# An L2 pool over four neighbours: fp32 throughout, 63 KB input runs in two slots, and the last stores queued behind the last load

## The chip, the cores and the metric

The kernel runs on one core of a Trainium2 chip. The metric is the device time of one execution in microseconds (us), the median of nine runs. ACT, DVE and SP stand for ScalarE, VectorE and SyncE; the core's 16 DMA engines move all data between device memory and SBUF.

## The reference

For x of shape 32 x 256 x 4096 in fp32, p = 2 and a window of 4, each output is the root of the mean of the squares of four neighbours along the last axis:

```python
for i in range(out_length):
    window = np.abs(x[:, :, i * 4:i * 4 + 4]) ** p
    result[:, :, i] = (np.mean(window, axis=-1)) ** (1.0 / p)
```

The input is 134.2 MB, the output (32 x 256 x 1024) 33.55 MB. Each byte is moved once.

## The kernel before

The input is seen as 8192 rows of 4096. The loop at L46 makes 32 tiles of 256 rows, two consecutive rows for each of the 128 partitions, so one partition's part of a tile is one run of 8192 elements (32 KB). The load of a tile (L50, 4 MB) is issued on SP's queue into one of three slots of `in_pool` (L42): the load of tile i + 3 waits on SP until the second square of tile i has read its slot.

A tile is worked in two halves of 4096 columns (L56). For each half ACT squares fp32 into bf16 (L60). DVE then adds in two steps: elements 0 and 1 of each group of four to elements 2 and 3 (L66, 2048 results in bf16, in `c`), then the two partial sums (L73, 1024 results, in `sum4`). ACT takes the root with the scale 1/4 (L78) into the fp32 output tile `ot`. After both halves the store of the tile (L84, 1 MB, 8 KB a partition) is issued on ACT's own queue, from one of four slots of `out_pool` (L44).

The order of instructions on each engine is set by the tile framework's scheduler from the program order and the dependencies. The trace shows the squares of a tile ahead of the root of the half before them where data are there. Two queues of DMA descriptors feed the same 16 engines: q1 holds SP's loads and q10 ACT's stores.

Of the kernel before, what the change touches and what calls it, by code (L numbers as in the profile page):

```python
# [1 line left out]

# [4 lines left out]


@with_exitstack
def kernel(  # L10
    ctx: ExitStack,
    tc: tile.TileContext,
    x: bass.AP,
    p: float,
    kernel_size: int,
    out: bass.AP,
):
    nc = tc.nc

    assert float(p) == 2.0, "kernel specialized for p == 2"  # L20
    k = int(kernel_size)
    assert k == 4, "kernel specialized for kernel_size == 4"

    x_flat = x.flatten_outer_dims()
    out_flat = out.flatten_outer_dims()
    R, L = x_flat.shape
    P = nc.NUM_PARTITIONS

    ROWS_PER_PART = 2
    CHUNK_ROWS = P * ROWS_PER_PART  # L30
    CL = L * ROWS_PER_PART
    CLo = CL // k
    assert R % CHUNK_ROWS == 0
    n_tiles = R // CHUNK_ROWS
    n_halves = 2
    HL = CL // n_halves
    HLo = HL // k

    fp32 = mybir.dt.float32
    bf16 = mybir.dt.bfloat16  # L40

    in_pool = ctx.enter_context(tc.tile_pool(name="in_pool", bufs=3))  # L42
    mid_pool = ctx.enter_context(tc.tile_pool(name="mid_pool", bufs=4))
    out_pool = ctx.enter_context(tc.tile_pool(name="out_pool", bufs=4))  # L44

    for i in range(n_tiles):  # L46
        rows = slice(i * CHUNK_ROWS, (i + 1) * CHUNK_ROWS)

        xt = in_pool.tile([P, CL], fp32)
        nc.sync.dma_start(  # L50
            out=xt,
            in_=x_flat[rows].rearrange("(p t) l -> p (t l)", t=ROWS_PER_PART),
        )

        ot = out_pool.tile([P, CLo], fp32)
        for h in range(n_halves):  # L56
            xh = xt[:, h * HL:(h + 1) * HL]

            x2 = mid_pool.tile([P, HL], bf16)
            nc.scalar.activation(  # L60
                out=x2, in_=xh, func=mybir.ActivationFunctionType.Square,
            )

            x2v = x2.rearrange("p (n j) -> p n j", j=k)
            c = mid_pool.tile([P, 2 * HLo], bf16)
            nc.vector.scalar_tensor_tensor(  # L66
                out=c.rearrange("p (n j) -> p n j", j=2),
                in0=x2v[:, :, 0:2], scalar=1.0, in1=x2v[:, :, 2:4],
                op0=mybir.AluOpType.mult, op1=mybir.AluOpType.add,
            )  # L70
            cv = c.rearrange("p (n j) -> p n j", j=2)
            sum4 = mid_pool.tile([P, HLo], bf16)
            nc.vector.scalar_tensor_tensor(  # L73
                out=sum4, in0=cv[:, :, 0], scalar=1.0, in1=cv[:, :, 1],
                op0=mybir.AluOpType.mult, op1=mybir.AluOpType.add,
            )

            nc.scalar.activation(  # L78
                out=ot[:, h * HLo:(h + 1) * HLo], in_=sum4,
                func=mybir.ActivationFunctionType.Sqrt,  # L80
                scale=1.0 / k,
            )

        nc.scalar.dma_start(  # L84
            out=out_flat[rows].rearrange("(p t) l -> p (t l)", t=ROWS_PER_PART),
            in_=ot,
        )


# [1 line left out]
_INS = ['x', 'p', 'kernel_size']  # L91
_OUTS = [((32, 256, 1024), 'float32')]
#: Inputs that are plain numbers.
_NUMBERS = {'p': 2.0, 'kernel_size': 4}


# [26 lines left out]
```

## Time and profile before

| what | value |
|---|---|
| median of 9 runs (lowest to highest) | 404.66 us (404.59 to 405.06) |
| the profiled execution: its time / its span | 404.75 us / 402.8 us |
| moved, and mean rate over the span | 167.80 MB, 417 GB/s |
| loads (L50): number, size, median from issue to landing | 32, 4096 KB, 28.3 us |
| stores (L84): number, size, median from issue to landing | 32, 1024 KB, 16.6 us |
| SP's queue waiting for ACT's squares (L60), in total | 228.6 us, 29 times |
| ACT idle ahead of the squares, for loads | 58.8 us |
| DVE idle ahead of the first add, for squares | 170.5 us |

A row of an instruction group reads: line, engine, operation, tile written <- tile read, shapes and types, number of instructions | busy time in all (us) and mean of one (ns) | idle time of the engine just ahead of them, and what ended it. A row of a busy-time table reads: the stretch and its length (us), busy time and instructions of DVE, ACT and POOL, the granted clock, the mean share of time in which a DMA engine held a packet, and GB/s. In the row of slices each digit is a fortieth of the span, 9 for 90% or more.

### The profile page before, as it was taken

The numbers are of one execution on the slowest core, as the hardware profiler recorded it, in microseconds if no ns is written. First come the engines' busy times: TensorE is split into PE (matmuls) and PEld (weight loads), VectorE is DVE, ScalarE is ACT, GpSimd is POOL, SyncE is SP. The second block draws the span as 40 slices with busy tenths as digits, with TensorE's granted clock in tenths as the row PEclk, the third lists the DMA queues.
The fourth block names the chain that finished last, engine by engine and source line by source line (L and its number), as shares of the span: only waits on it lengthen the run. The fifth ranks groups of instructions, "written<-read, shape, count | busy, mean of one in ns | idle before, by whom it ended". The sixth has DMA issues, their size and how long they took to land.

```text
span 402.8 us, 424 instructions
## 1 busy us (share of the span) xinstructions
DVE 224.3 (56%) x128; ACT 293.0 (73%) x130; POOL 0.2 (0%) x4
## 2 busy tenths in 40 slices
DVE  0357466645556654466554566455566554566454
ACT  1788777787676885767977677876767977677872
POOL 0000000000000000000000000000000000000000
DMA  8999999999999999999999999999999999999962
GB/s 355 426 428 405 443 446 403 440 456 403 456 413 433 443 434 423 451 402 448 438 414 448 422 428 448 432 418 451 404 446 440 417 443 432 418 448 414 430 257 104
DMA packets 9219, 167.80 MB, mean 417 GB/s; under 512 B 1024, under 2 KB 1024, under 8 KB 1024
## 3 DMA queue, kind: packets, MB, share of 16 engines
q1 hardware_dynamic: 4608, 134.22, 77.4%
q10 hardware_dynamic: 4608, 33.56, 19.7%
q14 instruction: 3, 0.02, 0.0%
HBM read 134.22 MB, written 33.55 MB: 416 GB/s over the span
## 4 chain that ended last, share of the span: by engine, by line
DMA 58%; ACT 26%; DVE 9%; issue 6%; SPq 0%; ACTq 0%
DMA xt<-in_x_dram 58%; ACT x L60 22%; DVE c L66 6%; ACT ot L78 4%; DVE sum L73 3%; SPq L50 0%; ACTq L78 0%
## 5 line engine op out<-in xcount | busy, mean ns | idle before, releaser
L60 ACT ACTIVATE x<-xt 128x4096 bf16<-128x4096 f32 x64 | 229.1, 3604 | 58.8 <-DMA xt<-in_x_dram 58.8
L66 DVE SCALAR_TENSOR_TENSOR c<-x 128x2048 bf16<-128x2048 bf16 x64 | 146.7, 2292 | 170.5 <-ACT x L60 170.5
L78 ACT ACTIVATE ot<-sum 128x1024 f32<-128x1024 bf16 x64 | 67.1, 1049 | 45.5 <-DVE sum L73 43.8
L73 DVE SCALAR_TENSOR_TENSOR sum<-c 128x1024 bf16<-128x1024 bf16 x64 | 78.4, 1225 | 2.2
L60 ACT ACT_TABLE_LOAD x1 | 1.3, 1283 | 0.7 <-PEq L104 0.7
L78 ACT ACT_TABLE_LOAD x1 | 1.3, 1283 | 0.0
L104 POOL MEMSET const-bfloat16-1.0<- 128x1 bf16 x1 | 0.1, 101 | 0.0
L104 POOL MEMSET const-uint8-127<- 128x1 uint8 x1 | 0.1, 101 | 0.0
L104 POOL MEMSET const-float32-0.0<- 128x1 f32 x1 | 0.1, 98 | 0.2 <-issue 0.2
L104 POOL MEMSET const-float32-1.0<- 128x1 f32 x1 | 0.1, 98 | 0.0
## 6 DMA issues: line engine op xcount, KB each, us to landing
xt<-in_x_dram SPq DMA_DIRECT2D x32, 4096.0 KB, 28.3
out_dram<-ot ACTq DMA_DIRECT2D x32, 1024.0 KB, 16.6
```

Source lines behind the costliest of these rows:

```text
L60: nc.scalar.activation(out=x2, in_=xh, func=mybir.ActivationFunctionType.Square,)
L66: nc.vector.scalar_tensor_tensor(out=c.rearrange("p (n j) -> p n j", j=2), in0=x2v[:, :, 0:2], scalar=1.0, in1=x2v[:, :, 2:4], op0=mybir.A ...
L73: nc.vector.scalar_tensor_tensor(out=sum4, in0=cv[:, :, 0], scalar=1.0, in1=cv[:, :, 1], op0=mybir.AluOpType.mult, op1=mybir.AluOpType.add,)
L78: nc.scalar.activation(out=ot[:, h * HLo:(h + 1) * HLo], in_=sum4, func=mybir.ActivationFunctionType.Sqrt, scale=1.0 / k,)
L104: nc = _bacc.Bacc("TRN2", target_bir_lowering=False, num_devices=1)
```

## The change

The work is laid out anew over the flat input, 262144 elements for each of the 128 partitions.

- Fourteen big tiles of W = 16128 elements a partition (63 KB, one run each, 8.26 MB) go through two slots of `x_pool`. Two big tiles share one block of device memory, so that they have one output tile `ot` of 8064 elements a partition (32 KB) and one store of 4.13 MB.
- What is left, 36352 elements a partition, is the tail: four loads of H = 8064 elements (two to a slot) and one of END = 4096. The last load takes the slot of the first two, which must be worked off first; in the unused part of that slot lie the outputs of the last two groups.
- Everything is fp32. Squares and roots are taken in place. Of a big tile's four column blocks of CH = 4032, ACT squares three and a half and DVE half of the fourth (a plain multiply). DVE's two adds are plain tensor_tensor additions through a small scratch tile `s`.
- `manual_schedule` keeps the order of the program text on every engine. In it all squares of a big tile come first, then the adds, then the load of the tile after next (SP), then two roots of 2016 elements, and after every second big tile the store, on ACT's queue. In the tail the root of a block comes after the square of the next.
- The store of the last pair of big tiles and the two stores of the tail are issued on SP's queue, after the last load.

The diff, blank lines left out:

```diff
-    x_flat = x.flatten_outer_dims()
-    out_flat = out.flatten_outer_dims()
-    R, L = x_flat.shape
     P = nc.NUM_PARTITIONS
-    ROWS_PER_PART = 2
-    CHUNK_ROWS = P * ROWS_PER_PART
-    CL = L * ROWS_PER_PART
-    CLo = CL // k
-    assert R % CHUNK_ROWS == 0
-    n_tiles = R // CHUNK_ROWS
-    n_halves = 2
-    HL = CL // n_halves
-    HLo = HL // k
     fp32 = mybir.dt.float32
-    bf16 = mybir.dt.bfloat16
-    in_pool = ctx.enter_context(tc.tile_pool(name="in_pool", bufs=3))
-    mid_pool = ctx.enter_context(tc.tile_pool(name="mid_pool", bufs=4))
-    out_pool = ctx.enter_context(tc.tile_pool(name="out_pool", bufs=4))
-    for i in range(n_tiles):
-        rows = slice(i * CHUNK_ROWS, (i + 1) * CHUNK_ROWS)
-        xt = in_pool.tile([P, CL], fp32)
+    Act = mybir.ActivationFunctionType
+    Alu = mybir.AluOpType
+    xf = x.rearrange("b c l -> (b c l)")
+    of = out.rearrange("b c l -> (b c l)")
+    total = xf.shape[0] // P
+    CH = 4032
+    W = 4 * CH
+    H = W // 2
+    BIG = 14
+    END = total - BIG * W - 4 * H
+    assert END == 4096
+    x_pool = ctx.enter_context(tc.tile_pool(name="x_pool", bufs=2))
+    o_pool = ctx.enter_context(tc.tile_pool(name="o_pool", bufs=2))
+    s_pool = ctx.enter_context(tc.tile_pool(name="s_pool", bufs=2))
+    ctx.enter_context(tc.manual_schedule())
+    def block(flat, first, width):
+        return flat[first * P:(first + width) * P].rearrange("(p w) -> p w", p=P)
+    def square_act(v):
+        nc.scalar.activation(out=v, in_=v, func=Act.Square)
+    def square_dve(v):
+        nc.vector.tensor_tensor(out=v, in0=v, in1=v, op=Alu.mult)
+    def root(o):
+        nc.scalar.activation(out=o, in_=o, func=Act.Sqrt, scale=1.0 / k)
+    def add1(v):
+        s = s_pool.tile([P, CH // 2], fp32, name="s")
+        n = v.shape[1]
+        vv = v.rearrange("p (n j) -> p n j", j=4)
+        nc.vector.tensor_tensor(
+            out=s[:, 0:n // 2].rearrange("p (n j) -> p n j", j=2),
+            in0=vv[:, :, 0:2], in1=vv[:, :, 2:4], op=Alu.add,
+        )
+        return s[:, 0:n // 2]
+    def add2(o, s):
+        sv = s.rearrange("p (n j) -> p n j", j=2)
+        nc.vector.tensor_tensor(out=o, in0=sv[:, :, 0], in1=sv[:, :, 1], op=Alu.add)
+    xts = {}
+    def load(i):
+        xt = x_pool.tile([P, W], fp32, name="xt")
         nc.sync.dma_start(
-            out=xt,
-            in_=x_flat[rows].rearrange("(p t) l -> p (t l)", t=ROWS_PER_PART),
+            out=xt, in_=block(xf, i // 2 * 2 * W, 2 * W)[:, i % 2 * W:(i % 2 + 1) * W],
         )
-        ot = out_pool.tile([P, CLo], fp32)
-        for h in range(n_halves):
-            xh = xt[:, h * HL:(h + 1) * HL]
-            x2 = mid_pool.tile([P, HL], bf16)
-            nc.scalar.activation(
-                out=x2, in_=xh, func=mybir.ActivationFunctionType.Square,
-            )
-            x2v = x2.rearrange("p (n j) -> p n j", j=k)
-            c = mid_pool.tile([P, 2 * HLo], bf16)
-            nc.vector.scalar_tensor_tensor(
-                out=c.rearrange("p (n j) -> p n j", j=2),
-                in0=x2v[:, :, 0:2], scalar=1.0, in1=x2v[:, :, 2:4],
-                op0=mybir.AluOpType.mult, op1=mybir.AluOpType.add,
-            )
-            cv = c.rearrange("p (n j) -> p n j", j=2)
-            sum4 = mid_pool.tile([P, HLo], bf16)
-            nc.vector.scalar_tensor_tensor(
-                out=sum4, in0=cv[:, :, 0], scalar=1.0, in1=cv[:, :, 1],
-                op0=mybir.AluOpType.mult, op1=mybir.AluOpType.add,
-            )
-            nc.scalar.activation(
-                out=ot[:, h * HLo:(h + 1) * HLo], in_=sum4,
-                func=mybir.ActivationFunctionType.Sqrt,
-                scale=1.0 / k,
-            )
-        nc.scalar.dma_start(
-            out=out_flat[rows].rearrange("(p t) l -> p (t l)", t=ROWS_PER_PART),
-            in_=ot,
-        )
+        xts[i] = xt
+    tail_at = BIG * W
+    tail = [(tail_at + j * H, H) for j in range(4)] + [(tail_at + 4 * H, END)]
+    three = block(xf, tail_at, 3 * H)
+    two = block(xf, tail_at + 3 * H, H + END)
+    tail_src = [three[:, 0:H], three[:, H:2 * H], three[:, 2 * H:3 * H], two[:, 0:H], two[:, H:]]
+    tail_x = {}
+    def load_tail(js):
+        xt = x_pool.tile([P, W], fp32, name="xt")
+        at = 0
+        for j in js:
+            w = tail[j][1]
+            nc.sync.dma_start(out=xt[:, at:at + w], in_=tail_src[j])
+            tail_x[j] = xt[:, at:at + w]
+            at += w
+        return xt
+    load(0)
+    load(1)
+    ot = None
+    for i in range(BIG):
+        xt = xts[i]
+        if i % 2 == 0:
+            ot = o_pool.tile([P, 2 * W // k], fp32, name="ot")
+        base = i % 2 * W // k
+        c = [xt[:, j * CH:(j + 1) * CH] for j in range(4)]
+        o = [ot[:, base + j * CH // k:base + (j + 1) * CH // k] for j in range(4)]
+        square_dve(c[3][:, 0:CH // 2])
+        square_act(c[0])
+        square_act(c[1])
+        square_act(c[2])
+        square_act(c[3][:, CH // 2:CH])
+        s0 = add1(c[0])
+        add2(o[0], s0)
+        s1 = add1(c[1])
+        add2(o[1], s1)
+        s2 = add1(c[2])
+        s3 = add1(c[3])
+        add2(o[2], s2)
+        add2(o[3], s3)
+        if i + 2 < BIG:
+            load(i + 2)
+        elif i + 2 == BIG:
+            load_tail((0, 1))
+        else:
+            load_tail((2, 3))
+        root(ot[:, base:base + 2 * CH // k])
+        root(ot[:, base + 2 * CH // k:base + W // k])
+        if i % 2 == 1 and i < BIG - 1:
+            nc.scalar.dma_start(out=block(of, (i - 1) * W // k, 2 * W // k), in_=ot)
+    ot_pair = ot
+    ot_three = o_pool.tile([P, 2 * W // k], fp32, name="ot")
+    ot_two = None
+    pending = None
+    for j in range(5):
+        if j == 2:
+            last_x = load_tail((4,))
+            ot_two = last_x[:, END:END + (H + END) // k]
+        w = tail[j][1]
+        step = CH if w == H else w // 2
+        for c in range(0, w, step):
+            v = tail_x[j][:, c:c + step]
+            square_act(v)
+            s = add1(v)
+            at = (j * H + c) // k if j < 3 else ((j - 3) * H + c) // k
+            o = (ot_three if j < 3 else ot_two)[:, at:at + step // k]
+            add2(o, s)
+            if pending is not None:
+                root(pending)
+            pending = o
+    root(pending)
+    nc.sync.dma_start(out=block(of, (BIG - 2) * W // k, 2 * W // k), in_=ot_pair)
+    nc.sync.dma_start(out=block(of, tail_at // k, 3 * H // k), in_=ot_three[:, 0:3 * H // k])
+    nc.sync.dma_start(out=block(of, (tail_at + 3 * H) // k, (H + END) // k), in_=ot_two)
```

## The prediction

> **What bounds the kernel now.** I read the page's slices first, then its DMA queues, then the stretches at the end, and only then the instruction groups.
>
> ```profile
> span 402.8 us, 424 instructions
> ...
> DVE 224.3 (56%) x128; ACT 293.0 (73%) x130; POOL 0.2 (0%) x4
> ...
> DMA  8999999999999999999999999999999999999962
> ...
> q1 hardware_dynamic: 4608, 134.22, 77.4%
> q10 hardware_dynamic: 4608, 33.56, 19.7%
> ```
>
> No engine is full, but the DMA row is at 9 from the second slice to the 38th: the 16 DMA engines always have work. The two queues together hold them for 97.1% of the span, 391.1 us. What is left, 11.7 us, is where time can be had. The busy-time table of five stretches shows where it lies (the last two columns are DMA share and GB/s):
>
> ```profile
> 40.00:380.00 340.00, 196.45 (x113) 254.11 (x113) 0.00 (x0) 1.00 1.00 432
> ...
> 385.00:390.00 5.00, 0.37 (x2) 4.62 (x3) 0.00 (x0) 1.00 0.79 326
> 390.00:399.00 9.00, 6.97 (x4) 5.57 (x3) 0.00 (x0) 1.00 0.00 1
> 399.00:402.80 3.80, 0.00 (x0) 0.00 (x0) 0.00 (x0) 1.00 0.67 276
> ```
>
> From 40 to 380 us the DMA share is 1.00 at 432 GB/s. From 390 to 399 us nothing moves. The chain of waits in order of time says why: the last tile has landed, and everything after it is serial.
>
> ```profile
> 386.44 3.51 ACT x L60
> 389.95 0.02 issue
> 389.98 2.30 DVE c L66
> 392.28 0.02 issue
> 392.31 1.23 DVE sum L73
> 393.53 2.26 DVE c L66
> 395.79 0.02 issue
> 395.81 1.24 DVE sum L73
> 397.05 0.02 issue
> 397.07 1.06 ACT ot L78
> ```
>
> Only then is the last store issued (398.16 us), which lands 3.9 us later. The rows from which I cost the work:
>
> ```profile
> L60 ACT ACTIVATE x<-xt 128x4096 bf16<-128x4096 f32 x64 | 229.1, 3604 | 58.8 <-DMA xt<-in_x_dram 58.8
> L66 DVE SCALAR_TENSOR_TENSOR c<-x 128x2048 bf16<-128x2048 bf16 x64 | 146.7, 2292 | 170.5 <-ACT x L60 170.5
> L78 ACT ACTIVATE ot<-sum 128x1024 f32<-128x1024 bf16 x64 | 67.1, 1049 | 45.5 <-DVE sum L73 43.8
> L73 DVE SCALAR_TENSOR_TENSOR sum<-c 128x1024 bf16<-128x1024 bf16 x64 | 78.4, 1225 | 2.2
> ```
>
> **Durations after.** ACT: L60 and L78 give (3604-1049)/3072 = 0.832 ns an element and 0.2 us fixed; one that follows another starts 0.1 us early (L60s in a row start 3.51 us apart). So a square of 4032 takes 3.55 us (3.45 in a row), of 2016 1.77, of 2048 1.8; a root of 2016 takes 1.87, of 1008 1.04. No row has fp32 both in and out, but L60 reads fp32 and L78 writes it at this rate, so I take no surcharge. DVE: L66 and L73 give 1.042 ns an element and 0.158 us: 2.26 us for the first add or the half square (2016), 1.21 us for the second add (1008).
>
> This is where the skill speaks against the change. "VectorE: DVE Perf Modes", § The perf-mode tier table, gives bf16 tensor_tensor twice the rate of fp32. If L66 ran at that doubled rate, fp32 would cost twice the row: 16.1 us of DVE per big tile (2.26 + 4x2.26 + 4x1.21) would become some 31, against about 24 us of DMA per tile, and DVE would be the bound at near 500 us. But the row shows 2292 ns for 2048 elements, one per 1.1 ns: the bf16 form was already at the single rate, so there is nothing to lose. The other warning is in "SBUF — State Buffer", § Specifications: reads need at least two hits in each 16-byte line for full rate. Both fp32 adds take two of the four words of a line, exactly two hits, where bf16 had four. The row shows no loss at four; no row shows two. Below the row it can't go (twice the bytes); above, I bound it at twice the row and take the row, as the page asks for two.
>
> **Part 1, descriptors.** By the queue lines a load packet of 32 KB took 0.774 x 402.8 x 16 / 4096 = 1.218 us, a store packet of 8 KB 0.310 us (semaphore packets spread in). The line through both is 0.0370 ns a byte and 0.007 us fixed. After, loads go in 63 KB runs and stores in 32 KB: up to the landing of the last big tile each engine has some 160 data descriptors for 410, 250 x 0.007 = 1.8 us less. Nothing larger than 32 KB is in the trace; the gain lies between 0 and 1.8, I take 0.9. (Were 63 KB pieces handled at the 8 KB rate, loads would cost 2.5%, about 6 us more; the trend of the rows is the other way.)
>
> **Part 2, two slots.** Take T as the landing of a big tile. Its successor already streams: 8.26 MB take 19.1 us alone, 28.7 when a 4.13 MB store shares (I assume that pieces of 63 and 32 KB alternate, so the load gets two thirds; another share moves landings about, not the sum). The load after that waits on SP for this slot. ACT squares end at T+12.2 (3.55 + 2x3.45 + 1.77). DVE: half square to 2.26, adds of c0 from 3.6 to 7.0, of c1 to 10.5, first adds of c2 and c3 to 15.0, where the slot is free. The issue follows at once, and the first packet about 1.0 us later (before: issue 0.73, packets from about 1.6), so T+16. The successor's packets run until T+18.2 (it landed at T+19.1, packets end about 0.9 earlier). The margin is 2 us without a store and over 10 with one: no gap in the steady state. ACT's second root waits for the last add and ends at T+19.3, then the store is issued (0.34 on ACT's queue), with the next tile's squares behind both: at most 0.6 us late, and only ahead of the store-loaded interval. ACT has 16 us and DVE 16.1 us of work in a mean interval of 24: hidden.
>
> **Part 3, the end.** Landing of the last big tile: loads 0 to 13 and six stores less a remainder, 140.2 MB, at 432 GB/s 324.6 us; plus 1.8 us start, 0.6 us for the slower first slices, 0.5 us to the semaphore, less 0.9: 326.5 us, my zero from here. The tail loads land at 10.1, 19.7, 29.2, 38.8. ACT is held by the second root to 19.3; then squares and roots alternate, and the fourth 4032 square ends at 35.25, its first add at 37.55. Only then is the slot of the last load (2.1 MB) free: data flow at 38.7, where the queue ran dry at 37.9. The gap is 0.8 us. On SP the stores of the last pair and of the three wait behind this load; their data are ready (19.3 and 49.7). Load to 43.6, pair store (4.13 MB) to 53.1, three (3.1 MB) to 60.3: these cover the compute that lay bare before. ACT goes on: squares 4 to 7 end at 53.1, the two of 2048 at 59.5, then add, add, root: 62.1. The last store (1.56 MB) takes 3.6 + 1.5 (before: 3.9 for 1.05 MB, of which 2.4 is data): 67.2; then 0.75 us to the end of the span, as before (402.06 to 402.8). Gap at the last store: about 2.9 us. Span 326.5 + 67.2 + 0.75 = 394.4.
>
> In short: 10 us of idle DMA become under 4, the store behind the last chain grows a little, descriptors save about 1. The profiled run took 404.75 us with a span of 402.8, so 1.95 us lie around the span; that run is 0.1 above the median. **394.4 + 1.95 = 396.4 us.**
>
> **Rivals.**
> - *All descriptor gain, shorter end:* the whole 1.8 us and no gaps before the last store give 392.7 to 394.5. For: the line through the two packet sizes. Against: nothing shown above 32 KB. 393.5 us, chance 0.10.
> - *The slot margin is thin:* DVE adds 24% dearer, or a slower wait on SP, use up the 2 us, and each of 7 intervals without a store gets a gap near 0.7 us. 399 to 403, say 401 us. For: two-hit reads, untried here. Chance 0.12.
> - *Slower, by DVE's strided fp32 reads:* with a factor f on the adds the slot is free at 3.55 + 11.46 f; packets stop for 11.46 (f - 1.18) in each of 7 intervals. At f = 1.28 this is 8 us, all that was won; beyond, it is slower than before. At f = 1.5: 26 us there and 6 in the DVE-bound end, 428 us. For: the two-hit limit is met exactly. Against: L66's element rate shows no penalty. Chance 0.05.
> - *It doesn't overlap as written:* squares by DVE and ACT in place in one tile are ordered as a whole, not by columns, so adds start after all squares: free at 2.26 + 12.2 + 11.5 = 26, a gap of 8.9 us in 7 intervals, near 460 us. The trace has no in-place write to tell. Chance 0.03.
>
> **How the numbers follow.** Forecast 396.4 (394.5 to 398.5) has 0.70. A run tells some 0.2% from no change. Faster: 0.70 + 0.10 + nearly all of 0.12, 0.91; within 0.2%: 0.01; slower 0.08. The range 392.8 to 402 holds the forecast, the better case and most of the thin-margin one, and leaves out some 0.12.
>
> **What would show it.** Right: the DMA row at 9 up to the last two or three slices, no stretch of several us without traffic; loads' packets near 2.4 us (queue share of loads about 79% of a shorter span); first add near 2260 ns, fp32 square near 3550; the wait of SP for DVE long before the queue is dry; last root some 5.8 us before the end. Wrong: first adds over 2.9 us, DMA share under 0.97 in the middle, the first add of c0 starting after all squares, or a dry queue before the last load of more than 2 us.

## The result, and the profile after

The changed kernel takes 401.17 us (median of 10 runs, 400.26 to 402.54) against 404.74 us beside it, a ratio of 0.9914 (95% interval 0.9906 to 0.9922). It is faster by 3.6 us, where 8.3 were forecast. Its runs also scatter more than those of before, by 0.6% instead of 0.1%. The profiled execution took 400.68 us with a span of 398.9 us.

From the page of the changed kernel, the lines that answer to those of before:

```profile
span 398.9 us, 388 instructions
...
DVE 252.1 (63%) x146; ACT 265.3 (67%) x106; POOL 0.2 (0%) x4
...
DMA  9999999999999999999999999999999999998997
...
q1 hardware_dynamic: 3168, 143.00, 84.5%
q10 hardware_dynamic: 864, 24.77, 14.4%
...
L58 ACT ACTIVATE xt<-xt 128x4032 f32<-128x4032 f32 (+1 forms) x66 | 203.5, 3144 | 81.2 <-DMA xt<-in_x_dram 81.2
...
L61 DVE TENSOR_TENSOR xt<-xt 128x2016 f32<-128x2016 f32 x14 | 31.6, 2258 | 107.8 <-DMA xt<-in_x_dram 107.8
```

The idle end is gone: the DMA row is at 8 or 9 up to the slice before the last. But look at the two queue lines. Packets hold the engines for 98.9% of 398.9 us, 394.5 us, where the same bytes took 391.1 us before and the prediction counted on 0.9 us less. Idle time of the DMA engines fell by 7.3 us (11.7 to 4.4), and 3.4 us of it went into packets that take longer.

The end itself, in the timeline of the changed kernel (start, length, engine and line):

```profile
331.26 12.24 ACT L58 ACTIVATE xt<-xt 128x4032 f32<-128x4032 f32 x4 [9.13 <-DMA xt<-in_x_dram]
...
348.46 1.88 ACT L64 ACTIVATE ot<-ot 128x2016 f32<-128x2016 f32 x1 [3.18 <-DVE ot L78]
...
392.22 0.63 ACT L64 ACTIVATE xt<-xt 128x512 f32<-128x512 f32 x1 [1.50 <-DVE xt L78]
392.87 0.33 SPq L167 DMA_DIRECT2D out_dram<-xt  x1
```

The last big tile has landed at 331.26 us. The span ends 67.6 us later; the prediction had 67.95. So the end runs as worked out, ACT setting its pace, and the whole error lies ahead of it: this landing was put at 326.5.

Where the packets take longer is seen in the busy-time table of the changed kernel. The stretches are chosen around the issues of the six pair stores; the last two columns are DMA share and GB/s:

```profile
58.00:67.00 9.00, 5.29 (x3) 7.60 (x3) 0.00 (x0) 1.00 1.01 398
67.00:92.00 25.00, 13.64 (x9) 13.12 (x6) 0.00 (x0) 1.00 1.01 437
...
106.00:115.00 9.00, 4.62 (x3) 7.61 (x3) 0.00 (x0) 1.00 1.07 459
...
154.00:163.00 9.00, 4.63 (x4) 6.44 (x3) 0.00 (x0) 1.00 0.95 373
163.00:188.00 25.00, 14.23 (x9) 13.03 (x6) 0.00 (x0) 1.00 1.01 436
...
202.00:212.00 10.00, 5.62 (x4) 7.36 (x3) 0.00 (x0) 1.00 0.99 413
...
250.00:261.00 11.00, 6.60 (x5) 8.09 (x3) 0.00 (x0) 1.00 0.95 375
...
299.00:309.00 10.00, 5.60 (x4) 7.83 (x3) 0.00 (x0) 1.00 0.93 381
```

The share stays at 0.93 to 1.01 while the rate falls to 373 to 398 GB/s at four of the six starts (413 at a fifth, no fall at 106 to 115 us): the engines hold a packet, but it moves slowly. In the trace's packet records a 63 KB load packet takes 2.38 us at the median, yet many around these places take 2.5 to 3.7 us. In what follows, **stretch** is the time of packets beyond the median of their size, summed and divided by 16 engines. Up to the end of the last big load it is 4.7 us, 0.84 of it at the very start. (In the kernel before, the whole run has 1.2 us.)

### The profile page after: what moved, and what is told of

Its sections match the earlier page's. It is cut to its first block, busy times and chain, and to the rows that moved or that the text cites. A ratio compares the mean times of both kernels' runs of the same rounds, so it can differ in the third digit from the quotient of the medians.

```text
span 398.9 us, 388 instructions
## 1 busy us (share of the span) xinstructions
DVE 252.1 (63%) x146; ACT 265.3 (67%) x106; POOL 0.2 (0%) x4
## 4 chain that ended last, share of the span: by engine, by line
DMA 56%; DVE 22%; ACT 16%; issue 5%; DVEq 0%; ACTq 0%
DMA xt<-in_x_dram 56%; DVE s L70 15%; ACT xt L58 13%; DVE ot L78 6%; ACT ot L64 2%; DVE xt L78 0%; ACT xt L64 0%; DVEq L70 0%; ACTq L64 0%
## 5 line engine op out<-in xcount | busy, mean ns | idle before, releaser
L58 ACT ACTIVATE xt<-xt 128x4032 f32<-128x4032 f32 (+1 forms) x66 | 203.5, 3144 | 81.2 <-DMA xt<-in_x_dram 81.2
L70 DVE TENSOR_TENSOR s<-xt 128x2016 f32<-128x2016 f32 (+1 forms) x66 | 145.7, 2225 | 31.0 <-ACT xt L58 31.0
L61 DVE TENSOR_TENSOR xt<-xt 128x2016 f32<-128x2016 f32 x14 | 31.6, 2258 | 107.8 <-DMA xt<-in_x_dram 107.8
L64 ACT ACTIVATE ot<-ot 128x2016 f32<-128x2016 f32 (+1 forms) x34 | 58.7, 1726 | 43.3 <-DVE ot L78 43.1
L78 DVE TENSOR_TENSOR ot<-s 128x1008 f32<-128x1008 f32 x62 | 73.5, 1205 | 1.2
L64 ACT ACTIVATE xt<-xt 128x1008 f32<-128x1008 f32 (+1 forms) x4 | 3.3, 828 | 2.3 <-DVE xt L78 2.3
L78 DVE TENSOR_TENSOR xt<-s 128x1008 f32<-128x1008 f32 (+1 forms) x4 | 3.8, 950 | 0.1
```

The lines of the kernel that those rows point to most:

```text
L58: nc.scalar.activation(out=v, in_=v, func=Act.Square)
L61: nc.vector.tensor_tensor(out=v, in0=v, in1=v, op=Alu.mult)
L64: nc.scalar.activation(out=o, in_=o, func=Act.Sqrt, scale=1.0 / k)
L70: nc.vector.tensor_tensor(out=s[:, 0:n // 2].rearrange("p (n j) -> p n j", j=2), in0=vv[:, :, 0:2], in1=vv[:, :, 2:4], op=Alu.add,)
L78: nc.vector.tensor_tensor(out=o, in0=sv[:, :, 0], in1=sv[:, :, 1], op=Alu.add)
```

## The experiments

Theory A at the outset: each start of a store stretches the loads beside it. Theory B: the 63 KB pieces do. Theory C: two queues that alternate make the engines drift apart. A fourth, D, came out of the runs. The first four ran beside 404.68 us for the kernel before.

**Single stores.** The edit:

```diff
-        if i % 2 == 1 and i < BIG - 1:
-            nc.scalar.dma_start(out=block(of, (i - 1) * W // k, 2 * W // k), in_=ot)
+        if i < BIG - 2:
+            nc.scalar.dma_start(
+                out=block(of, i // 2 * 2 * W // k, 2 * W // k)[:, base:base + W // k],
+                in_=ot[:, base:base + W // k],
+            )
```

> Each of the first twelve big tiles is stored by itself (2.06 MB, 16 KB a partition) on ACT's queue, in place of six pair stores. Theory A (each start of a store beside running loads stretches a load packet on all engines by some 0.6 us, seen as about 3.5 us in six starts): twelve starts, 3 us more, near 404 us. Theory B (the 63 KB load pieces are the cost): unchanged, 401 us, or a little less. Theory C (a drift of the engines by whole store pieces, up to 2.5 us at the last landings): shorter pieces, less drift, about 400 us.

Measured 397.67 us (ratio 0.983, 0.9817 to 0.9843). Twice the starts, and faster: theory A as put is wrong. The gain was also larger than B or C had it.

**Halved loads.**

```diff
-        nc.sync.dma_start(
-            out=xt, in_=block(xf, i // 2 * 2 * W, 2 * W)[:, i % 2 * W:(i % 2 + 1) * W],
-        )
+        src = block(xf, i // 2 * 2 * W, 2 * W)[:, i % 2 * W:(i % 2 + 1) * W]
+        for h in range(2):
+            nc.sync.dma_start(out=xt[:, h * H:(h + 1) * H], in_=src[:, h * H:(h + 1) * H])
```

> Each 63 KB load is issued as two loads of 31.5 KB a partition, into the same slot and with the same waits. Theory B (the long pieces): 3 us or more come back, 396 to 398 us. Theory A (starts of stores): the starts stay, 401 to 402 us (112 more pieces at 0.008 us). Theory C (drift): perhaps 1 us less, 400 us.

Measured 397.21 us (0.9819, 0.9806 to 0.9833), inside what B gives. This kernel keeps the six starts and the long idle time of the store queue ahead of each, and only the first still costs anything:

```profile
58.00:67.00 9.00, 6.05 (x4) 8.55 (x4) 0.00 (x0) 1.00 0.99 401
...
154.00:163.00 9.00, 5.89 (x4) 8.59 (x4) 0.00 (x0) 1.00 1.02 441
202.00:212.00 10.00, 6.95 (x4) 9.59 (x4) 0.00 (x0) 1.00 1.05 452
250.00:261.00 11.00, 8.18 (x5) 10.58 (x4) 0.00 (x0) 1.00 1.03 446
```

**Stores on SP's queue.** `nc.scalar.dma_start` of the pair store becomes `nc.sync.dma_start`, at the same place in the text.

> The six pair stores are issued on SP's queue behind the next load, not on ACT's: loads and stores no longer share the engines piece by piece but follow one another. Theory A: the starts stay and stretch the last load packets ahead of them, about 401 us. Theory C (alternation of two queues makes the engines drift): 397 to 399 us. Theory B: 401 us.

Measured 396.31 us (0.9793, 0.978 to 0.9807), below all three. Taken for itself it comes nearest to C. It has 63 KB loads throughout, and from the fifth on they are hardly stretched (0.20 us an engine at most), which B can't have.

**The end alone.** The tiles, types and input slots of before. Besides the end, the order is fixed by `manual_schedule`, ACT's root of a half comes behind the next square, and there are six output slots and not four. The lines of the end (cut out of a larger edit):

```diff
+    tiles = [(i * CHUNK_ROWS, 2) for i in range(n_tiles - 1)]
+    tiles += [((n_tiles - 1) * CHUNK_ROWS, 1), ((n_tiles - 1) * CHUNK_ROWS + P, 1)]
...
+        if last and i < n_tiles - LATE:
+            store(nc.scalar, i, ot)
+        elif last:
+            late.append((i, ot))
...
+    for i, ot in late:
+        store(nc.sync, i, ot)
```

> The kernel before, in its tiles of 32 KB runs, bf16 and three slots, with the end alone changed: the last tile is loaded in two halves and the stores of the last four tiles lie on SP's queue behind the last load. The steady state then has no stretched packets: 391 us of packets plus about 1.8 us at the start and 1.2 us at the end and little in between, span 394 to 395, 396 to 397 us. If the end were not what the gain is made of (the rival: gaps only move), 402 us or more.

Measured 400.5 us (0.9895, 0.9881 to 0.9908), 4 us above what I expected. The end, with the order that goes with it, is worth 4.2 us. The table of its last stretches says why not 8:

```profile
385.00:389.00 4.00, 2.87 (x4) 4.00 (x4) 0.00 (x0) 1.00 0.97 403
389.00:393.00 4.00, 3.23 (x4) 3.83 (x4) 0.00 (x0) 1.00 0.38 154
393.00:396.00 3.00, 1.26 (x2) 0.63 (x1) 0.00 (x0) 1.00 0.07 30
```

ACT is busy almost without a break while the DMA engines run dry from 390 us. The tile ahead lands at 373.1 us and the two halves at 378.0 and 382.9. The tile ahead keeps ACT for some 9 us, so that it takes up the first half at 382.1 only, and it has both to work off until 395 us. I had counted only the chain of the last half. The stretch is 1.2 us, as before.

All runs from here on ran beside 404.67 us for the kernel before.

**The change once more,** without an edit.

> The changed kernel itself, without an edit, beside the others of this call. If the first comparison holds: 400 to 402.5 us, load packets stretched by about 3.5 us in all around the starts of its six pair stores. If its 401 us belonged to that chip and hour alone: 397 to 398 us, as all three variants gave, and then their gain is not from their edits.

Measured 400.85 us (0.9907, 0.9891 to 0.9923), stretch 4.0 us up to the last big load. The gains above are of their edits. In the profile (401.89 us) the last big tile lands earlier, at 330.15 us, but the end takes 69.95 us, since one of the 16 engines finishes the last store 1.9 us behind all others.

**Halved stores.** The pair store at its old place and time, as two DMAs of 16 KB pieces:

```diff
-            nc.scalar.dma_start(out=block(of, (i - 1) * W // k, 2 * W // k), in_=ot)
+            dst = block(of, (i - 1) * W // k, 2 * W // k)
+            for h in range(2):
+                half = slice(h * W // k, (h + 1) * W // k)
+                nc.scalar.dma_start(out=dst[:, half], in_=ot[:, half])
```

> Each pair store at the same place and time, but as two DMAs of 16 KB pieces (the load keeps its 63 KB pieces). Theory B2 (long load pieces and long store pieces together on two queues stretch the loads): about 397.5 us, as with single stores per tile. Theory A2 (what matters is that the store queue has lain idle for some 18 us before each store): unchanged, 401 us.

Measured 395.07 us (0.9763, 0.975 to 0.9775), the best of all: 9.6 us under the kernel before and 5.8 under the change once more. Its page and its table:

```profile
span 393.0 us, 394 instructions
...
DMA  9999999999999999999999999999999999999997
...
202.00:212.00 10.00, 5.76 (x4) 7.14 (x3) 0.00 (x0) 1.00 1.02 440
...
250.00:261.00 11.00, 7.17 (x4) 8.54 (x3) 0.00 (x0) 1.00 1.05 455
...
299.00:309.00 10.00, 7.55 (x4) 8.92 (x3) 0.00 (x0) 1.00 1.00 434
```

Both theories of my expectation give part of this, since the edit did two things. The pieces of the two queues alternate one for one in the records. So halving the store's pieces about halves its rate: eight pieces last as long as eight of the load, 23.8 us (8 x (2.38 + 0.60)), and the store is now spread over two intervals and not over one. From 63 to 338 us the store queue is never idle, and tiles land every 23.8 us and not by turns after 20 and 28. Between the profiled spans lie 5.9 us: 4.8 of stretch (2.8 up to the last big load, 1.9 at the last load of 2 MB) and 1.6 of idle time, less 0.4 for twice as many store pieces. The next two runs take these apart.

**No stores in the middle.** The two lines of the pair store are taken out.

> The six stores of the first twelve big tiles are left out, so those outputs are missing; loads, squares, adds, roots and the end stay. 24.77 MB less, 57.3 us of store packets. If stores cost only their packets: the changed kernel's time less 57.3. If each also stretches the loads and makes the engines drift: 4 to 5 us less than that, near 339.5 us from 401.2; some 2 us of it may be lost again since ACT has 19.3 us of work for a tile that now lands every 19.1.

Measured 342.09 us (0.8461, 0.8448 to 0.8474). The change less 57.3 us of store packets is 343.5 (from 400.85), so 1.5 us came back, not 4 to 5. At the landing of the last big tile it was more: 272.84 us for 331.26 are 58.4 less, and the 46 of 48 store pieces an engine that had gone by then account for 54.9. The other two lay behind the landing, where ACT sets the pace and they cost nothing. The surprise is in the table (of a run of 343.57 us, 1.5 above the median, so that the others may have less of it):

```profile
60.00:190.00 130.00, 107.18 (x61) 110.44 (x42) 0.00 (x0) 1.00 1.00 431
190.00:300.00 110.00, 86.45 (x51) 89.23 (x35) 0.00 (x0) 1.00 0.99 424
```

With no store at all, loads are stretched from about 190 us on, though by less: 0.1 to 0.5 us an engine in each of the last four. A store is not needed for that. ACT does not fall behind: the half square starts with the landing, and the next load is issued 15 us later, at the start as near the end:

```profile
42.04 2.26 DVE L61 TENSOR_TENSOR xt<-xt 128x2016 f32<-128x2016 f32 x1 [1.88 <-DMA xt<-in_x_dram]
57.00 0.33 SPq L85 DMA_DIRECT2D xt<-in_x_dram  x1
...
233.93 2.26 DVE L61 TENSOR_TENSOR xt<-xt 128x2016 f32<-128x2016 f32 x1 [1.83 <-DMA xt<-in_x_dram]
248.94 0.33 SPq L85 DMA_DIRECT2D xt<-in_x_dram  x1
```

What grows on the way is the distance between the engines. The first and the last of the 16 finish the fourth load 1.1 us apart, the thirteenth 2.3. A landing follows the last engine, while the packets of a load begin on the first, so the time between issue and first packet shrinks.

**Half of each store.** As the halved stores, with `range(1)`.

> Of each of the six pair stores only the first half of the columns is stored, in 16 KB pieces, so half the outputs of the first twelve big tiles are missing. 12.4 MB less. The store queue is idle again for over 20 us ahead of each start. Theory A (a start on an idle queue stretches 63 KB loads, whatever the store's pieces): the rate falls to 370 to 415 GB/s in the ten us around each of the six starts, some 3 us in all, 370 to 372 us. Theory B (32 KB store pieces stretch them): 428 GB/s or more around all starts but the first, 366.5 us (395.1 less 28.6).

Measured 372.95 us (0.9221, 0.9194 to 0.9247), 1 us above what A gave, 6 above B. With the same 16 KB pieces as the best kernel, and fewer of them, the middle runs slower (in a run of 375.02 us, 2 above the median):

```profile
60.00:302.00 242.00, 173.35 (x99) 175.55 (x67) 0.00 (x0) 1.00 1.00 422
```

against 433 and 432 GB/s from 50 to 200 and from 200 to 320 us with halved stores. The store's piece length (B) is out. A has the time, but not quite the place: around the six starts the rate is 373, 419, 459, 413, 463 and 414 GB/s, and after the first it is lowest over the 20 us behind a start (390 and 393). A start on an idle queue is also not enough, since the halved loads have five without stretch, nor needed for all of it, as the run without stores shows.

**Both halved:** the two edits together.

> Loads in 31.5 KB pieces and each pair store as two DMAs of 16 KB pieces, on ACT's queue. If the two edits cure one and the same thing, the stretched packets: 395 us, as the halved stores alone. If halved loads cure something else as well (the engines' drift): 394 us or less.

Measured 397.23 us (0.9815, 0.9802 to 0.9829), 2 us slower than halved stores alone, which neither view had. The middle is well (432 GB/s from 60 to 320 us); the end is not:

```profile
320.00:365.00 45.00, 28.61 (x17) 32.68 (x14) 0.00 (x0) 1.00 1.00 430
365.00:375.00 10.00, 7.72 (x5) 10.00 (x5) 0.00 (x0) 1.00 0.97 339
```

The last big tile lands at 328.8 us, 5 us later than with halved stores alone (323.9): there, more store bytes are still waiting at that moment and cover the end later. Here ACT sets the end again, the load of the last 2 MB comes too late, and it is stretched.

**Halved loads with stores on SP's queue.**

> Both edits that helped: loads in 31.5 KB pieces, and the pair stores on SP's queue behind the next load. If they cure two things: 394 to 395.5 us, under either one. If they cure the same thing: 396 to 397 us, as either alone.

Measured 396.57 us (0.9799, 0.9786 to 0.9812), as under either alone: by their times the two cure the same thing.

**Theory D, the lead of a load.** What the stretched loads of the change share is that SP issued them late. In the changed kernel, the issue, the store behind it and the landing of the load ahead (L61 starts with it):

```profile
153.19 0.33 SPq L85 DMA_DIRECT2D xt<-in_x_dram  x1
157.35 0.34 ACTq L140 DMA_DIRECT2D out_dram<-ot  x1
158.44 2.26 DVE L61 TENSOR_TENSOR xt<-xt 128x2016 f32<-128x2016 f32 x1 [3.03 <-DMA xt<-in_x_dram]
```

And with half of each store, where the lead is shorter still:

```profile
189.29 0.33 SPq L85 DMA_DIRECT2D xt<-in_x_dram  x1
191.54 0.34 ACTq L143 DMA_DIRECT2D out_dram<-ot  x1
193.43 2.26 DVE L61 TENSOR_TENSOR xt<-xt 128x2016 f32<-128x2016 f32 x1 [1.93 <-DMA xt<-in_x_dram]
```

From the packet records, the lead (issue to first packet, us) and the stretch of the same load (us an engine). The big loads 4 to 13 are meant (the first of each two, where loads are halved), or the loads named:

```
the change          lead 11.8  4.0 12.3  2.5 10.3  2.7 10.3  2.4 10.5  2.7
                 stretch    0 0.21 0.03 0.85    0 0.39    0 0.86    0 0.54
half of each store  lead  8.2  1.9  7.3  1.4  6.9  1.2  7.1  1.5  7.0  1.7
                 stretch    0 0.70 0.03 1.03 0.07 1.21    0 0.95    0 0.83
no stores           lead  2.6  2.6  2.3  2.3  2.0  2.0  2.1  2.0  1.6  2.2
                 stretch 0.08 0.02 0.03    0 0.02 0.11 0.30 0.17 0.52 0.11
halved stores       all leads 7.2 to 7.8    all stretches under 0.07
single stores       all leads 7.0 to 7.7    all stretches under 0.07
halved loads        leads 4.1 to 14.3       all stretches under 0.07
stores on SP        leads 10 to 13          stretches up to 0.20
last 2 MB load, the change: queue dry, lead 1.0, stretch 1.85
```

In these kernels no load issued 7 us ahead or more lost over 0.2 us. Those issued 1 to 3 us ahead of their packets lost up to 1.2 us. But the lead is not all. Without stores, loads 4 to 9 had leads of 2.0 to 2.6 us and lost 0.11 us at most; in the change four loads with leads of 2.4 to 2.7 lost 0.39 to 0.86. And there the loss lies at the store: of the 3.7 us in its loads 3, 5, 7, 9, 11 and 13, 3.3 us are in two packets an engine, the last load packet ahead of the store's first piece and the first one behind it. So in the change most of it is a late load and the start of a store together. The five later starts of the halved loads, at leads of 4.1 to 4.7, cost nothing.

The last 2 MB load shows the lead with no store on the other queue. In seven profiles it was issued 1.0 us ahead and lost 1.8 to 2.1 us, also in the two with halved loads and stores on ACT's queue, where the engines stood idle for only 0.2 us ahead of it. With halved stores (4.0 us ahead) and in the two kernels with stores on SP's queue (5.2 and 7.0) it lost 0.02 us or less.

All three kinds of cure lengthen the lead. Stores that last two intervals make the short interval 24 us long. A store in the loads' own queue stands between a load and the next. Halved loads are still issued together, but sooner behind the landing, 13.4 to 13.8 us instead of 15, since the first half is worked on before the second is there:

```profile
108.85 2.26 DVE L61 TENSOR_TENSOR xt<-xt 128x2016 f32<-128x2016 f32 x1 [3.46 <-DMA xt<-in_x_dram]
...
122.68 0.99 SPq L87 DMA_DIRECT2D xt<-in_x_dram  x2
```

What I did not try is to delay the loads of the best kernel and leave the rest alone. So a short lead, worst where a store starts, is what fits all twelve profiles, and not yet what a single edit has proved. Why a late load is slow although its engine has other packets to move also stays open.

## Why the prediction was right and wrong

**What bounds the kernel: right.** The gap of 9 us was filled, and with the halved stores the span is 393.0 us, close to what the packets alone need.

**Durations: right.** A row of squares takes 12.24 us (forecast 12.2), the half square 2258 ns (2260), first adds 2.26 us. Two hits in a 16-byte line were enough for full rate, as the Trainium skill's "SBUF — State Buffer", § Specifications, says: the strided adds take as long as the contiguous half square of 2016. The doubling feared from its "VectorE: DVE Perf Modes", § The perf-mode tier table, did not come. The table sets fp32 tensor_tensor against bf16 tensor_tensor, and the rows before were of scalar_tensor_tensor, which it doesn't list; its 2293 ns for 2048 fp32 elements agrees with 2258 ns for 2016. The rival by DVE's strided reads and the one of a whole-tile order fall: the first adds start 3.6 us after the landing.

**Part 2, two slots: the sum was right, the conclusion wrong.** The slot of the first tile is free and the next load issued 14.96 us after its landing (22.72 to 37.68; forecast 15.0). The store-free interval leaves some 2 us, and no gap appears, as forecast. The step that failed is "The margin is 2 us without a store and over 10 with one: no gap in the steady state", since I took no gap for no cost. In the sum of Part 3 it is the term of 0.6 us for slow packets, which measured 4.7 (0.84 of it at the very start, as foreseen). The packets got slower before the queue ran dry, at six loads issued 2.4 to 4.0 us ahead, 0.2 to 0.9 us each, and three ways of lengthening that lead took the loss away. That the lead is the cause, and how, was not shown by a single edit.

My rival "the slot margin is thin" had nearly the place (six of its seven intervals) and the time (401 us), but dearer adds or a slower wait as its cause. The adds were as forecast and the issue came on time, so its number is luck in part: much of the delay is the drift of the engines and the late semaphore, which it did not have.

**Part 3, the landing of the last big tile: 326.5 forecast, 331.26 measured.** The terms in the packet records: 139.2 MB at the median time of the packets 321.3 us an engine, idle 1.5, stretch 4.7, the slowest engine 2.2 behind the mean, 1.2 until its semaphore packet (a store piece goes first) and 0.4 to DVE: 331.3. I had 0.6 for slow packets (4.1 too little) and 0.5 to the semaphore, with no drift of the engines at all (3.3 too little). At the landing the first and the last of the 16 engines finish 3.7 us apart, where it was 1.1 before. On the other side, fewer bytes had been moved by then, and packets at their median are faster than 432 GB/s, 2.4 us together. Theory C's drift is thus real, but a second queue is not what decides: halving the stores brought it to 1.8 us with both queues, and with loads alone it grew to 2.3.

**Part 1, descriptors: the line was right, and the whole gain came** (I took half, 0.9 of 1.8 us). The median packets of 63 and 31.5 KB take 2.380 and 1.194 us. With those of 32 and 8 KB before (1.213 and 0.309), all lie on one line of 0.0078 us plus 0.0368 us for 1000 bytes. (By the prediction's own rows, pieces at the 8 KB rate would have cost 1.8%, not 2.5%; its 6 us is right.)

**The end: right in sum.** 67.6 us for 67.95. Inside it the engines stood idle for 1.3 us ahead of the last load (0.8 forecast) and the packets after that lost 1.85 us, but ACT's chain ends last, so neither counted. The repeat of the change needed 69.95 us, for the one late engine at its last store.

**The total.** 396.4 + 4.8 (landing) - 0.3 (end) is 400.9 us, beside 400.68 of the profiled run and 401.17 of the median.

## What to carry to other kernels

A DMA share of 1.00 doesn't say that the engines run at full rate: read GB/s beside it, stretch by stretch, and compare the shares of the queues for the same bytes. With two slots, look at the shortest interval, not the mean one: here equal spacing was worth some 3 us with single stores, and 5.8 with halved ones, where the last load also came in time, with not a byte less. When work is put behind the last load to cover an end, count all that the slowest engine has left at that moment, not only the chain of the last piece.

## What the runs showed of the hardware that I had not expected

- Pieces of two queues alternate one for one in all five pairs of sizes looked at (32 and 8 KB, 63 and 32, 63 and 16, 31.5 and 32, 31.5 and 16), so a DMA's rate beside another is set by its piece length: beside 63 KB loads the 4.13 MB store takes 26.3 to 27.5 us from its first packet to its last in 32 KB pieces, and each 2.06 MB half of it 22 us in 16 KB pieces.
- A load issued 1 to 3 us ahead of its packets can lose up to 1.2 us, as the mean of the engines, with the DMA share still at 0.93 to 1.01. In the change this happens where a store starts. The last 2 MB load, issued 1.0 us ahead, lost 1.8 to 2.1 us with no store beside it.
- A load's semaphore waits behind a store piece on the same engine: 1.2 us for a 32 KB piece.
- The engines drift apart even with loads alone on one queue (1.1 to 2.3 us over nine loads), and a tile lands with the last of them.
- The first store of a kernel stretches loads by 0.3 to 0.9 us in all profiles that have one, that of before too (0.45 us at 24 to 32 us).
